# Splitting seventeen weight blocks of the second layer early, and writing the order of every engine out

## The chip, the cores and the metric

The kernel runs on one core of one Trainium2 chip. The metric is the device time of one execution in microseconds, lower is better. The core has five engines that work side by side, each through its own queue in order: TensorE (PE; its weight loads are listed apart as PEld), VectorE (DVE), ScalarE (ACT), GpSimd (POOL) and SyncE (SP), which here issues the transfers. An instruction starts when its engine reaches it and the results that it needs are there.

## The reference

A decoder trunk of two layers on 1024 tokens of 1024 features, all in float32. Each layer has a mixer stage and a feed-forward stage:

```python
for l in range(DEPTH):
    h = rmsnorm(x, attn_norm[l])
    proj = h @ w_in[l]
    (c_q, c_kv, k_r, g_b, g_c, u_conv, u_pool,
     q_sw, k_sw, v_sw) = jnp.split(proj, pts, axis=-1)
    y_a = mla_attention(c_q, c_kv, k_r, ..., w_uq[l], w_ukv[l], cos, sin)
    y_b = short_gated_conv(g_b, g_c, u_conv, conv_w[l])
    y_c = multiscale_pool(u_pool, pool_w[l], pool_scale[l])
    y_d = swa_sink_attention(q_sw, k_sw, v_sw, swa_sinks[l], slopes)
    gf = ... # each group divided by its own root mean square
    x = x + (gf * mix_norm[l]) @ w_o[l]
    h2 = rmsnorm(x, ffn_norm[l])
    gate, up = jnp.split(h2 @ w_gate_up[l], 2, axis=-1)
    x = x + (jax.nn.silu(gate) * up) @ w_down[l]
return rmsnorm(x, final_norm)
```

The four mixers are a latent attention (queries and keys from narrow latents, each with a norm of its own), a gated convolution, pooling over 2 to 16 tokens, and an attention over a window of 128 tokens ("local" below). d_ff is 2816.

## The kernel before

Activations lie transposed: features on the 128 partitions, tokens on the free axis, in two halves t of 512. TensorE is fed with numbers in a shorter format (fp32r), so each float32 operand is split into a high part and the remainder, and a product is three matmuls, high by high, high by low, low by high (`mm3`, line 294 issues them). Splitting is one copy on ACT (line 305, or 308 with a gain) and one subtract on DVE (306 or 309), over tiles of 512 or 1024 columns. Gate and up, down, and part of the input projection of layer 1 use a scheme with seven products of quarter blocks in place of eight. The combined quarters of weights and activations that it needs are worked out ahead on POOL and DVE and kept in DRAM (tiles ws, qd, ad).

The names of tiles in the rows: u is one of 47 slots of 128 x 1024, tn, tp and te are small work tiles, ps_ is PSUM, par holds per-feature gains. A number after a name is a version.

The mixers' weights are loaded in the order in which `expect_layer` lists them. `weights` (line 222) starts a load from the input, then ACT copies (line 237) and DVE subtracts (line 238), into a ring of two pairs of slots.

A norm, `rnorm`, is a chain over four engines: a matmul with ones sums the squares (line 355 or 358), then ACT does Ln (362), Exp (363) and Square (364), DVE corrects (365, 368) and multiplies the input (372), and the result is split (308, 309) and goes to PE. In ACT's queue an ACT_TABLE_LOAD stands ahead of an Ln, Exp or Silu wherever the table set loaded before it in that queue isn't the one for its function. The kernel itself asks for a set of Ln and Exp together, "natural_log_exp_and_others", at its start (line 151) and after each feed-forward (line 1828). The second statement depends on the Silu that the program emitted last:

```python
pl = act.preload_act_table_set("natural_log_exp_and_others")
if pl is not None:
    tc.add_manual_dep(pl.ins, last_silu.ins.name, ...)
```

`swa_unit` works out a block of local attention for two heads: scores in PSUM, maximum with the sink, an exponential on ACT (776), the row's reciprocal on DVE, the scaling of each head's tile by it (791, DVE, 128x256), then transposes and the product with the values.

The feed-forward's loop runs over 22 blocks of 128 gate and 128 up features. The first block is started ahead of the loop proper. `norm(u)` norms half u of the input; `combine` builds the quarters of the activations; `plain_gates`, `plain_silus` and `plain_acts` finish the first block, in plain products, with its Silu on ACT (line 1604) and its two multiplications on DVE. The down projection is a second loop, over 28 units.

What sets the order: the program emits everything in an order of its own, and then a planner (`arrange`) lays out every engine's queue. It goes by estimated durations, ranks and a table MOVES of offsets by line, and by one rule on tables: steps with Silu and steps with Exp or Ln are kept apart, all of one kind ahead of the other. The loads of tables are no steps of the planner; they are put in around its order.

Of the kernel before, what the change touches and what calls it, by code (L numbers as in the profile page):

```python
# [18 lines left out]
P = 128  # L19
# [27 lines left out]
NPL = 1  # L47

# [74 lines left out]
def trunk_kernel(ctx: ExitStack, tc: tile.TileContext, ins, out):  # L123
# [32 lines left out]
    ws = dpool.tile([len(PAIRS), P, 4 * 7 * NQ], F32, name="ws")  # L156
    ad = [dpool.tile([P, NG * HT], F32, name=f"ad{n}") for n in range(7)]
# [82 lines left out]

    def rope_weights(l):

        s = F.half()
        raw = F.ap(s)
        sp.dma_start(raw, ins["w_kr"][l])
        w = R.ap2(ring_next()[0])
        F.free(s)
        rv = raw.rearrange("p (k c) -> p k c", k=NK)
        wv = w.rearrange("p (k h c) -> p k h c", k=NK, h=2)
        act.copy(wv[:, :, 0], rv)  # L250
        dve.tensor_tensor(out=wv[:, :, 1], in0=rv, in1=rd(wv[:, :, 0]), op=ALU.subtract)
        return w
# [6 lines left out]
    def expect_layer(l):  # L259
        for m in (2, 3, 0, 4, 5, 6, 1, 13, 14, 10, 11, 12, None, 7, 8, 9) if l == 0 else (14, 10, 11, 12, None, 7, 8, 9):  # L260
            if m is None:
                expect(rope_weights, l)
            else:
                begin = [first_loads] if (l, m) == (0, 2) else []
                expect(weights, ins["w_in"][l, m], 2 * HT, *begin)
        for d in range(NK):
            expect(weights, ins["w_o"][l, d], 6 * P)
# [241 lines left out]

    factors = {c: [None] * (NK // 2) for c in USES}  # L510
# [65 lines left out]
    for l in range(L):  # L576
# [3 lines left out]
        prep = factor_weights() if l == 0 else iter(())  # L580

# [160 lines left out]
        def swa_unit(g, i):  # L742
# [747 lines left out]
        for n, (h, t) in enumerate(steps):  # L1490
# [27 lines left out]
            if n == 6:  # L1518
# [12 lines left out]
                for k in range(2):  # L1531
                    wa.append(pair_weights(ins["w_oa"][l, k]))
# [190 lines left out]
        combine(1)  # L1723
        plain_gates()
        plain_silus()
        plain_acts()
        norm(1)
# [16 lines left out]
        for f in range(NPL, NFF):  # L1744
# [76 lines left out]
            if f in range(4, 20, 2):  # L1821
                next(prep, None)
        second(*pending)
# [148 lines left out]
MM_NS = {512: 226.7, 384: 173.3, 256: 120.0, 128: 57.0}  # L1972
SIGNAL = {
    "PE": {"PE": 0, "DVE": 37, "ACT": 36, "POOL": 62, "SP": 30},
    "DVE": {"PE": 168, "DVE": 33, "ACT": 33, "POOL": 79, "SP": 27},
    "ACT": {"PE": 165, "DVE": 33, "ACT": 25, "POOL": 77, "SP": 26},
    "POOL": {"PE": 192, "DVE": 33, "ACT": 32, "POOL": 78, "SP": 27},
    "SP": {"PE": 163, "DVE": 35, "ACT": 35, "POOL": 80, "SP": 30},
}
REUSE = {"PE": 153, "DVE": 40, "ACT": 40, "POOL": 40, "SP": 40}  # L1980
OVERLAP = {"DVE": 82, "ACT": 97, "POOL": 44}
SHIFT = {"DVE": 31, "ACT": 24, "POOL": 0}
FUNC_SETS = {"Silu": "Silu", "Exp": "Exp", "Ln": "Exp"}
ENGINES = {"PE": "PE", "DVE": "DVE", "Activation": "ACT", "Pool": "POOL", "SP": "SP"}


class Step:
    __slots__ = ("ins", "eng", "rank", "before", "after", "tiles", "left", "ns", "tail", "ready", "sums", "bank", "onchip", "size", "start", "end", "table", "rows", "place")

    def __init__(self, eng, rank):  # L1990
        self.ins, self.eng, self.rank = [], eng, rank
        self.before, self.after, self.tiles = set(), [], []
        self.ns = self.tail = self.ready = self.size = 0
        self.sums = self.bank = None
        self.onchip = False
        self.table = self.rows = None


def areas(a):
    t = a.bass_ap  # L2000
    shape = [int(n) for n in t.tensor.shape]
    dims = [(int(s), int(n)) for s, n in a.ap]
    off = int(t.offset)
    name = t.tensor.name
    if type(t.tensor).__name__ == "DRamTensorHandle" or name.split("_")[0] in DRAM_TILES:
        row = shape[-1]
        starts, rows, span = [off // row], 1, 1
        for s, n in dims:
            if s == row:
                rows = n  # L2010
            elif s % row == 0 and s:
                starts = [b + k * (s // row) for b in starts for k in range(n)]
            else:
                span += s * (n - 1)
        c = off % row
        return name, [(b, b + rows, c, c + span) for b in starts]
    row = 1
    for n in shape[1:]:
        row *= n
    p, c = divmod(off, row)  # L2020
    span = 1 + sum(s * (n - 1) for s, n in dims[1:])
    return name, [(p, p + dims[0][1], c, c + span)]


DRAM_TILES = {"ws", "xs", "xp", "xr", "qd", "out"} | {f"ad{n}" for n in range(7)}
BUFS = {"ps_mm": 2, "ps_m0": 1, "ps_m1": 1, "ps_s": 3, "ps_t": 2, "ps_pv": 1, "te": 2, "tn": 3, "tp": 3, "vraw": 2, "vhi": 2, "vlo": 2, "sm1": 16, "sm2": 16, "sm16": 2}


def width(a):
    n = 1  # L2030
    for s, k in list(a.ap)[1:]:
        n *= int(k)
    return n


def length(eng, kind, i, ins, outs):
    n = max(width(a) for a in ins + outs)
    ps = any(a.bass_ap.tensor.name.startswith("ps_") for a in ins)
    if eng == "POOL":
        return 206 if kind == "InstMemset" else 177 + 2.18 * n  # L2040
    if eng == "ACT":
        if kind == "InstTensorCopy":
            return 157 + 0.84 * n if ps else 187 + 0.845 * n
        if len(outs) > 1:
            return 261 + 0.836 * n
        if len(ins) > 1 or "Copy" in str(i.func):
            return 261 + 0.836 * n if ps else 294 + 0.83 * n
        return 170 + 0.84 * n if ps else 195 + 0.845 * n
    if kind == "InstCustomDveAnt":
        return 220 + 1.02 * n + 58  # L2050
    if kind == "InstTensorScalarPtr" and not i.is_scalar_tensor_tensor:
        return 152 + 0.53 * n if n < 64 else 215 + 0.514 * n
    if kind == "InstTensorCopy":
        return 150 + 0.52 * n
    if kind == "InstTensorScalarPtr" and len(ins) > 2 and not ps:
        return 212 + 1.04 * n
    return 146 + 1.054 * n


def steps_of(tc):  # L2060
    steps, seen = [], {}
    table, runs = None, {"Silu": [], "Exp": []}
    for i in tc.nc.cur_bb.bb.instructions:
# [4 lines left out]
        ins = [a for a in i.ins if hasattr(a, "bass_ap")]  # L2068
        outs = [a for a in i.outs if hasattr(a, "bass_ap")]
        fp32 = kind == "InstMatmult" and "float32r" not in str(i.ins[1].dtype)  # L2070
        bank = outs[0].bass_ap.tensor.name
        v = steps[-1] if steps else None
        if not (fp32 and v and v.sums and v.bank == bank):
            v = Step(eng, len(steps))
            steps.append(v)
            v.bank, v.sums = bank, fp32
        v.ins.append(i)
        if eng == "PE":
            n = width(outs[0])
            if fp32:  # L2080
                one = i.ins[1].bass_ap.tensor.name.startswith("ones")
                v.ns += {512: 867, 256: 534, 128: 340}[n] if one else 108
                v.tail = 163 if one else 122
            else:
                v.ns = MM_NS[n]
                v.tail = 164 if n > 128 else 173
        elif kind == "InstDMACopy":
            v.size = 4
            for s, n in outs[0].ap:
                v.size *= int(n)  # L2090
            if eng == "POOL":
                v.ns, v.tail = 700, 4200
            elif eng == "ACT":
                v.ns, v.tail = 450, 2400
        else:
            v.ns = length(eng, kind, i, ins, outs)
            if not any(a.bass_ap.tensor.name.startswith("ps_") for a in ins + outs):
                v.onchip = kind != "InstMemset"
            if ins:
                v.rows = tuple(areas(a)[1][0][0] for a in (ins[0], outs[0]))  # L2100
            if eng == "ACT" and len(outs) > 1:
                v.tail = 61
        f = FUNC_SETS.get(str(getattr(i, "func", "")).split(".")[-1])
        if f:
            other = runs["Exp" if f == "Silu" else "Silu"]
            if f != table:
                table = f
                runs[f] = []
            v.before |= set(other)
            runs[f].append(v)  # L2110
            v.table = f
        for a, writes in [(a, False) for a in ins] + [(a, True) for a in outs]:
            name, rects = areas(a)
            if kind == "InstCustomDveAnt":
                rects = [(0, 1 << 30, 0, 1 << 30)]
            if name.startswith("in_"):
                continue
# [856 lines left out]
```

## Time and profile before

| what | value |
|---|---|
| median of 3 runs | 2030.23 us (2029.9 to 2032.06) |
| the profiled execution | 2030.46 us |
| its span, first to last instruction | 2028.2 us |
| granted TensorE clock | 0.998 |
| instructions | 26434 |

The stages in the profiled execution: layer 0's mixers up to about 400 us, its feed-forward to about 810 and its down projection to about 1000; then layer 1 in the same way, its mixers to about 1400. A row of the timeline gives start, length, engine, line, operation, output and inputs, and in brackets how long the engine sat idle before it and what released it. A row of a group gives count, busy time, mean length in ns of one, and idle time before them.

### The profile page before, as it was taken

To read this page: it belongs to the slowest core of one execution; us is meant where nothing else is said; L and a number is where in the kernel's file an instruction comes from. 1 tells how busy PE (TensorE), PEld (TensorE's weight loads), DVE (VectorE), ACT (ScalarE), POOL (GpSimd) and SP (SyncE) were. 2 spreads that over 40 slices of the span, in tenths; PEclk is the share of its full clock that TensorE was granted. 3 is DMA by queue.
4 is the path that set the end of the run, shared out by engine and by line. 5 is a ranking of instruction groups with operands and counts; after the bars stand their busy time and mean duration, and the time that the engine had idled before them with its cause. 6 is when DMAs were issued, how large, how long until landed. Compare 5 with 4: busy or idle time off the path is not lost.

```text
span 2028.2 us, 26434 instructions
## 1 busy us (share of the span) xinstructions
PE 2012.0 (99%) x9378; PEld 1669.8 (82%) x9378; DVE 1641.9 (81%) x2793; ACT 1027.3 (51%) x1803; POOL 195.0 (10%) x212
## 2 busy tenths in 40 slices
PE   9999999999999999999999999999999999999997
PEld 8887888888888888888888878887888888888887
DVE  7889989998888888755778999899877877786455
ACT  6557667753433344544545676667333333354343
POOL 0000000021212212000000000000212222120000
PEclk9999999999999999999999999999999999999999
DMA  5111223346676577866455113231644544498652
GB/s 185 45 37 37 78 83 116 120 156 219 209 231 223 207 238 254 301 226 211 134 163 172 37 45 96 98 128 58 218 143 153 174 162 143 136 319 291 188 191 88
DMA packets 163780, 320.19 MB, mean 158 GB/s; under 512 B 13248, under 2 KB 85056, under 8 KB 163648
## 3 DMA queue, kind: packets, MB, share of 16 engines
q1 hardware_dynamic: 163648, 318.51, 46.8%
q8 instruction: 73, 1.20, 0.2%
q14 instruction: 59, 0.48, 0.1%
HBM read 220.41 MB, written 98.04 MB: 157 GB/s over the span
## 4 chain that ended last, share of the span: by engine, by line
PE 91%; DVE 6%; ACT 1%; issue 1%; DMA 0%; SPq 0%; DVEq 0%; ACTq 0%
PE ps_mm L294 35%; PE ps_s L294 28%; PE ps_t L294 11%; PE ps_pv L294 8%; PE ps_pv L1289 2%; PE ps_t L1277 2%; DVE u L309 1%; DVE u L1408 1%; PE ps_s L1223 1%; PE ps_s L1224 1%; PE ps_s L1225 1%; PE ps_s L753 1%; PE ps_pv L814 1%; DVE u L346 1%; PE ps_mm L1109 1%
## 5 line engine op out<-in xcount | busy, mean ns | idle before, releaser
L294 PE MATMUL ps_mm<-u,u 128*128 128x512 f32 (+1 forms) x3402 | 875.0, 388 | 2.0 <-ACT u L305 1.1
L294 PEld LDWEIGHTS ps_mm<-u,u 128*128 128x128 f32 x3402 | 622.6, 188 | 127.1 <-issue 2.6
L294 PE MATMUL ps_s<-u,u 128*128 128x512 f32 x2628 | 674.0, 389 | 1.2 <-ACT u L305 1.0
L294 PEld LDWEIGHTS ps_s<-u,u 128*128 128x128 f32 x2628 | 492.4, 188 | 105.5 <-ACT u L305 1.7
L305 ACT CAST u<-u 128x1024 fp32r<-128x1024 f32 (+2 forms) x400 | 343.8, 881 | 438.2 <-PE ps_s L294 91.0
L306 DVE TENSOR_TENSOR u<-u,u 128x1024 fp32r<-128x1024 f32 (+2 forms) x400 | 412.5, 1049 | 165.1 <-ACT u L305 122.7
L294 PE MATMUL ps_t<-u,u 128*128 128x512 f32 (+1 forms) x1142 | 297.3, 377 | 0.0
L172 POOL TENSOR_TENSOR u<-u 128x256 f32<-128x256 f32 x176 | 188.8, 1074 | 773.4 <-DMA u<-in_w_dn 370.1
L294 PEld LDWEIGHTS ps_t<-u,u 128*128 128x128 f32 x1142 | 205.6, 188 | 40.4 <-issue 0.5
L294 PE MATMUL ps_pv<-u,u 128*128 128x512 f32 x696 | 194.2, 389 | 0.0
L294 PEld LDWEIGHTS ps_pv<-u,u 128*128 128x128 f32 x696 | 130.3, 188 | 27.5 <-issue 0.4
L1604 ACT ACTIVATE tp<-tp 128x512 f32<-128x512 f32 x84 | 53.0, 632 | 102.5 <-DVE tp L372 102.2
L458 ACT COPY tn<-ps_s 128x512 f32<-128x512 f32 x66 | 38.5, 584 | 99.0 <-PE ps_s L294 98.9
L1286 POOL MEMSET u<- 128x128 f32 x32 | 6.0, 215 | 853.4 <-DVE te L372 618.2
L305 ACT CAST u<-ps_t 128x512 fp32r<-128x512 f32 (+4 forms) x136 | 65.1, 505 | 44.7 <-PE ps_t L1277 27.9
L308 ACT ACTIVATE u<-u,par 128x512 fp32r<-128x512 f32 x100 | 69.4, 717 | 29.8 <-DVE u L372 11.1
L306 DVE TENSOR_TENSOR u<-ps_t,u 128x512 fp32r<-128x512 f32 (+4 forms) x136 | 76.3, 581 | 4.7 <-ACT u L305 3.8
L309 DVE SCALAR_TENSOR_TENSOR u<-u,par,u 128x512 fp32r<-128x512 f32 x100 | 72.4, 744 | 6.8 <-ACT u L308 6.7
L1605 DVE TENSOR_TENSOR tp<-tp,u 128x512 f32<-128x512 f32 x84 | 61.8, 740 | 11.5 <-ACT tp L1604 11.2
L340 ACT ACTIVATE tn<-u 128x512 f32<-128x512 f32 (+1 forms) x92 | 52.6, 594 | 31.0 <-DVE u L1882 17.6
L372 DVE TENSOR_TENSOR tp<-tp,u 128x512 f32<-128x512 f32 x80 | 57.7, 725 | 0.9
L1289 PE MATMUL ps_pv<-u,u 128*128 128x512 f32 (+2 forms) x184 | 52.0, 355 | 0.0
(220 smaller groups left out, 2160.9 us busy)
## 6 DMA issues: line engine op xcount, KB each, us to landing
u<-in_w_gu SPq DMA_DIRECT2D x88, 512.0 KB, 3.9
ad<-u SPq DMA_DIRECT2D x154, 256.0 KB, 2.8
u<-ad SPq DMA_DIRECT2D x70, 512.0 KB, 5.3
u<-in_w_dn SPq DMA_DIRECT2D x68, 512.0 KB, 4.6
qd<-u SPq DMA_DIRECT2D x44, 512.0 KB, 3.0
u<-qd SPq DMA_DIRECT2D x32, 512.0 KB, 4.2
u<-in_w_in SPq DMA_DIRECT2D x29, 512.0 KB, 3.5
u<-ws SPq DMA_DIRECT2D x28, 512.0 KB, 4.0
```

Source lines behind the costliest of these rows:

```text
L172: pool.tensor_tensor(out=o, in0=o, in1=u, op=ALU.add)
L294: pe.matmul(o, w, r, start=start and k == 0 and i == 0, stop=stop and k == n - 1 and i == 2, skip_group_check=again,)
L305: act.copy(hi, f)
L306: dve.tensor_tensor(out=lo, in0=f, in1=rd(hi), op=ALU.subtract)
L308: act.activation(hi, f, AF.Copy, scale=gain)
L309: dve.scalar_tensor_tensor(out=lo, in0=f, scalar=gain, in1=rd(hi), op0=ALU.mult, op1=ALU.subtract)
L340: act.activation(q, f, AF.Square)
L372: dve.tensor_tensor(out=o, in0=a, in1=b, op=ALU.mult)
L1277: pe.transpose(p[:, b * P : (b + 1) * P], pr[b][j // 4][:, (j % 4) * P : (j % 4 + 1) * P], ident,)
L1289: pe.matmul(py[:, c0:], v_of(j, h), R.ap(s)[:, c0:], start=j == 0 and n == 0, stop=j == nj - 1 and n == 1,)
L1604: last_silu = act.activation(g, g, AF.Silu)
L1605: dve.tensor_tensor(out=g, in0=g, in1=r, op=ALU.mult)
```

## The change

Five things change.

1. Seventeen weight blocks of layer 1's mixers (seven of the input projection, the eight of the output projection's first part and the two of its attention part) are no longer split where they are used. `ready_block` reads one, splits it with one copy on ACT and one subtract on DVE, and writes both parts to a DRAM tile wl. It is called for odd f from 3 to 19 in layer 0's feed-forward loop (nine blocks) and for odd n from 5 on in its down projection (eight). In layer 1 `ready_weights` loads the two parts ready-made, with two transfers instead of one.
2. The scaling in `swa_unit` is an ACT copy with a per-row scale instead of a DVE multiplication, in both layers.
3. `norm(1)` stands ahead of `plain_gates`, `plain_silus` and `plain_acts` instead of behind them.
4. The planner, its costs and its table are gone. The order of all five engines is written out as a list of places (ORDER), and `order_engines` makes each instruction follow the one before it in that list. The rule on tables goes with the planner, and table loads are still no part of the list.
5. `expect_layer` and the loading of the attention's output weights use `ready_weights` for layer 1.

The matmuls and their number are the same. Line 362 becomes 375, 363 becomes 376, 305 becomes 318, 1604 becomes 1639 and 1828 becomes 1865.

```diff
+READY = (14, 10, 11, 12, 7, 8, 9) + tuple(("o", d) for d in range(NK)) + (("a", 0), ("a", 1))
...
+    wl = dpool.tile([len(READY), P, 2 * D], F32, name="wl")
...
+    def ready_weights(k, n):
+        pair = ring_next()
+        for j, i in enumerate(pair):
+            sp.dma_start(rd(R.ap2(i)[:, :n]), wl[READY.index(k)][:, j * D : j * D + n])
+        return [R.ap2(i) for i in pair]
...
+            elif l:
+                expect(ready_weights, m, D)
...
+            if l:
+                expect(ready_weights, ("o", d), 6 * P)
+            else:
+                expect(weights, ins["w_o"][l, d], 6 * P)
...
+    def ready_block(k):
+
+        s = F.pair()
+        if isinstance(k, int):
+            src, n = ins["w_in"][1, k], D
+        elif k[0] == "o":
+            src, n = ins["w_o"][1, k[1]], 6 * P
+        else:
+            src, n = ins["w_oa"][1, k[1]], D
+        f = F.ap2(s)[:, :n]
+        sp.dma_start(f, src)
+        h = R.pair()
+        hi = R.ap2(h)[:, :n]
+        act.copy(hi, f)
+        dve.tensor_tensor(out=f, in0=f, in1=rd(hi), op=ALU.subtract)
+        for j, v in enumerate((rd(hi), f)):
+            sp.dma_start(wl[READY.index(k)][:, j * D : j * D + n], v)
+        R.free_pair(h)
+        F.free_pair(s)
...
             for h in range(2):
-                dve.tensor_scalar(
-                    out=p3[:, h, c0:],
-                    in0=p3[:, h, c0:],
-                    scalar1=rs[:, h : h + 1],
-                    scalar2=None,
-                    op0=ALU.mult,
+                act.activation(
+                    p3[:, h, c0:], p3[:, h, c0:], AF.Copy, scale=rs[:, h : h + 1]
                 )
...
         combine(1)
+        norm(1)
         plain_gates()
         plain_silus()
         plain_acts()
-        norm(1)
...
             if f in range(4, 20, 2):
                 next(prep, None)
+            elif blocks_due and f in range(3, 20):
+                ready_block(blocks_due.popleft())
...
+            elif blocks_due and n % 2:
+                ready_block(blocks_due.popleft())
...
+ORDER = {
+    "PE": """
+0 24:2 -26:2 24:2 -26:2 24 -25:2 66 -44 18 24 -25:2 23 -24:3 -24 44 -45:2 -27:3 67 -68:3 21 43
...
+def order_engines(tc):
+
+    info = mybir.DependencyInfo(mybir.DependencyClass.NoSync, mybir.DependencyReason.DATA)
+    queues = {}
+    for eng, _, _, ins in steps_of(tc):
+        queues.setdefault(eng, []).append(ins)
+    for eng, queue in queues.items():
+        places = list(listed(ORDER[eng]))
+        assert sorted(places) == list(range(len(queue)))
+        last = None
+        for n in places:
+            for i in queue[n]:
+                if last:
+                    tc.add_manual_dep(i, last, info, reason="issue order")
+                last = i.name
```

**Where the order moves instructions.** First ACT's queue before, at the start of layer 0's feed-forward; L1604 is the first Silu, L362 and L363 the Ln and Exp of norm(1).

```order
L305 CAST u18_4190<-tp_4176 128x512
L1604 ACT_TABLE_LOAD
L1604 ACTIVATE tp_4193<-tp_4193 128x512
L305 CAST u22_4281<-tp_4273 128x512
L362 ACT_TABLE_LOAD
L362 ACTIVATE tn_4204<-ps_pv_4198 128x512
L305 CAST u24_4292<-u42_3928 128x1024
L363 ACT_TABLE_LOAD
L363 ACTIVATE tn_4204<-tn_4204 128x512
L305 CAST u32_2203<-tp_4274 128x512
```

The same place of ACT's queue now, with L375 and L376 for Ln and Exp and L1639 for the Silu:

```order
L318 CAST u18_4191<-tp_4177 128x512
L318 CAST u24_4293<-u42_3929 128x1024
L375 ACTIVATE tn_4200<-ps_pv_4194 128x512
L376 ACTIVATE tn_4200<-tn_4200 128x512
L318 CAST u22_4282<-tp_4274 128x512
L1639 ACT_TABLE_LOAD
L1639 ACTIVATE tp_4207<-tp_4207 128x512
L318 CAST u32_2204<-tp_4275 128x512
```

Ln and Exp moved ahead of the Silu, and one load stands there where three stood, a fourth, for the next Silu, following further down.

Next the end of layer 0's feed-forward, ACT's queue before; L1828 is the load of the joint set of Ln and Exp.

```order
L1604 ACTIVATE tp_7349<-tp_7349 128x512
L305 CAST u46_7484<-u0_7412 128x1024
L305 CAST u17_7488<-u36_7354 128x512
L305 CAST u9_7553<-u14_7551 128x1024
L1604 ACTIVATE tp_7451<-tp_7451 128x512
L1828 ACT_TABLE_LOAD
L305 CAST u29_7547<-u12_7545 128x1024
```

And now, with L1865 for that load:

```order
L1639 ACTIVATE tp_7515<-tp_7515 128x512
L1865 ACT_TABLE_LOAD
L318 CAST u10_7692<-u41_7628 128x1024
L318 CAST u44_7633<-u21_7418 128x384
L318 CAST u8_7748<-u15_7687 128x1024
L1639 ACT_TABLE_LOAD
L1639 ACTIVATE tp_7413<-tp_7413 128x512
L318 CAST u26_7693<-u30_7565 128x384
```

The Silu that the program emits last (tp_7515) comes ahead of another one (tp_7413), the joint set is loaded between the two, and the Silu's set is loaded again behind it.

Last, the norms of the latents in layer 1, ACT's queue before:

```order
L305 CAST u22_10717<-te_10715 128x512
L362 ACTIVATE tn_10586<-ps_t_10580 128x512
L363 ACTIVATE tn_10586<-tn_10586 128x512
L364 ACTIVATE tn_10587<-tn_10586 128x512
L335 ACTIVATE u24_10668<-u24_10668 128x512
L362 ACTIVATE tn_10657<-ps_t_10655 128x512
L363 ACTIVATE tn_10657<-tn_10657 128x512
L364 ACTIVATE tn_10658<-tn_10657 128x512
```

And now:

```order
L318 CAST u4_10829<-te_10827 128x512
L375 ACT_TABLE_LOAD
L375 ACTIVATE tn_10698<-ps_t_10692 128x512
L376 ACT_TABLE_LOAD
L376 ACTIVATE tn_10698<-tn_10698 128x512
L377 ACTIVATE tn_10699<-tn_10698 128x512
L375 ACT_TABLE_LOAD
L375 ACTIVATE tn_10769<-ps_t_10767 128x512
L348 ACTIVATE u28_10780<-u28_10780 128x512
L376 ACT_TABLE_LOAD
L376 ACTIVATE tn_10769<-tn_10769 128x512
L377 ACTIVATE tn_10770<-tn_10769 128x512
```

The steps of the norms stand in the same sequence, and each Ln and each Exp has a table load ahead of it. Over the whole program ACT's queue holds 11 table loads before and 38 now: one at the start, three in layer 0 and 34 in layer 1, of which 32 belong to the 16 norms.

More of the change, by code (lines that the diff above doesn't have):

```diff
@@ L1 @@
-import heapq
 import math
@@ L1981 @@
[L1981 to L1996, printed above, removed]
@@ L1999, in areas @@
[L1999 to L2022, printed above, removed]
@@ L2025 @@
[L2025 to L2057, printed above, removed]
@@ L2060, in steps_of @@
+ENGINES = {"PE": "PE", "DVE": "DVE", "Activation": "ACT", "Pool": "POOL", "SP": "SP"}
+ORDER = {
+    "PE": """
[172 rows of a table added]
+""",
+    "DVE": """
[76 rows of a table added]
+""",
+    "ACT": """
[46 rows of a table added]
+""",
+    "POOL": """
+0:2 1 -2 2 -2 2 -2 2 -2 1:2 1 -2 1:6 4:2 -6 5 -6:2 4 -5 4:78 1 -2 2 -2 2 -2 1:2 1 -2 1:92
+""",
+    "SP": """
[24 rows of a table added]
+""",
+}
 def steps_of(tc):
-    steps, seen = [], {}
-    table, runs = None, {"Silu": [], "Exp": []}
+    steps = []
     for i in tc.nc.cur_bb.bb.instructions:
@@ L2077, in steps_of @@
[L2077 to L2094, printed above, removed]
-        else:
[L2096 to L2117, printed above, removed]
-            if name.split("_")[0] not in DRAM_TILES and name not in v.tiles:
-                v.tiles.append(name)
-            seen.setdefault(name, [])
-            for r, w, u in seen[name]:
-                cross = name.startswith("ps_") and w == writes
-                if cross or (w or writes) and any(
-                    x[0] < y[1] and y[0] < x[1] and x[2] < y[3] and y[2] < x[3]
-                    for x in r
-                    for y in rects
-                ):
-                    v.before.add(u)
-            seen[name].append((rects, writes, v))
```

197 lines of the change are left out of this document (20 added, 177 removed), and 847 rows, old and new, of tables (MOVES, ORDER).

## The prediction

> **What bounds the kernel now.** The page comes first: its span, the busy shares, ScalarE's slices and the chain by engine.
>
> ```profile
> span 2028.2 us, 26434 instructions
> PE 2012.0 (99%) x9378; PEld 1669.8 (82%) x9378; DVE 1641.9 (81%) x2793; ACT 1027.3 (51%) x1803; POOL 195.0 (10%) x212
> PE 91%; DVE 6%; ACT 1%; issue 1%; DMA 0%; SPq 0%; DVEq 0%; ACTq 0%
> ```
>
> TensorE (PE) is busy for 2012.0 of 2028.2 us and carries 91% of the chain. The change leaves the matmuls as they are, so a gain can only come out of the 16.2 us in which PE does nothing, head and tail of the kernel included. A loss has no such lid: wherever another engine delivers late, PE's idle time grows, and nothing later wins it back. So the question is how much room the other engines have, stage by stage. The next view is busy time by window, in layer 1's mixers (columns: length, then PE, weight loads, DVE, ACT, POOL, clock, DMA share, GB/s).
>
> ```profile
> 1130.00:1160.00 30.00, 30.00 (x172) 25.96 (x170) 29.66 (x89) 25.24 (x65) 0.00 (x0) 1.00 0.13 42
> 1160.00:1197.00 37.00, 37.00 (x158) 28.66 (x157) 35.30 (x61) 29.87 (x52) 0.00 (x0) 1.00 0.10 32
> 1197.00:1218.00 21.00, 20.61 (x98) 17.11 (x97) 21.00 (x40) 12.63 (x25) 0.57 (x2) 1.00 0.15 52
> 1218.00:1240.00 22.00, 21.30 (x106) 17.31 (x107) 22.00 (x52) 16.14 (x40) 0.00 (x0) 1.00 0.20 56
> ```
>
> VectorE (DVE) is full from 1197 to 1240, and PE loses 0.39 + 0.70 = 1.1 us there; two subtracts of weights, of the kind that the change moves away, lie on the chain of waits:
>
> ```profile
> 1201.77 1.21 DVE u L238
> 1217.91 0.86 DVE u L238
> ```
>
> ScalarE (ACT) has 37.00 - 29.87 = 7.1 us free from 1160 to 1197. That window holds the norms of the latent queries, keys and the neighbouring groups. The page's 51% for ACT says nothing about it.
>
> Then the start of layer 0's feed-forward on ACT's timeline (start, length), and PE at the same place and at the same place in layer 1:
>
> ```profile
> 407.73 0.63 ACT L1604 ACTIVATE tp<-tp 128x512 f32<-128x512 f32 x1
> 408.26 0.61 ACT L305 CAST u<-tp 128x512 fp32r<-128x512 f32 x1
> 408.89 1.28 ACT L362 ACT_TABLE_LOAD   x1
> 410.18 0.60 ACT L362 ACTIVATE tn<-ps_pv 128x512 f32<-128x512 f32 x1
> 410.68 1.04 ACT L305 CAST u<-u 128x1024 fp32r<-128x1024 f32 x1
> 411.74 1.28 ACT L363 ACT_TABLE_LOAD   x1
> 413.03 0.63 ACT L363 ACTIVATE tn<-tn 128x512 f32<-128x512 f32 x1
> 413.57 0.60 ACT L305 CAST u<-tp 128x512 fp32r<-128x512 f32 x1
> ```
> ```profile
> 412.58 0.61 PE L294 MATMUL ps_s<-u,u 128*128 128x512 f32 x2
> 414.22 2.14 PE L294 MATMUL ps_s<-u,u 128*128 128x512 f32 x8 [1.03 <-ACT u L305]
> ```
> ```profile
> 1413.28 0.39 PE L294 MATMUL ps_s<-u,u 128*128 128x512 f32 x1
> 1414.73 0.74 PE L294 MATMUL ps_mm<-u,u 128*128 128x512 f32 x2 [1.06 <-ACT u L305]
> ```
>
> This is what a change of function table costs. A 128x512 step normally starts 0.53 us after the one before it (407.73 to 408.26). With a load between them, the Ln starts 410.18 - 408.26 = 1.92 us after the cast: 1.4 us more, for a load of 1.28. After a Silu both Ln and Exp need a load of their own (408.89, 411.74), and the cast behind them reaches PE 1.03 us late. In layer 1's mixers before there is no such load; the view of line 362 (the Ln), from 960 to 1420 us, has one, at 1405.8, in the feed-forward, for 12 + 4 norms:
>
> ```profile
> L362 ACT ACTIVATE tn<-ps_t x12: 577/600/619, 1161.6 to 1352.7; 128x512 f32<-128x512 f32 x12
> L362 ACT ACTIVATE tn<-ps_pv x4: 575/583/599, 1002.4 to 1407.1; 128x512 f32<-128x512 f32 x4
> L362 ACT ACT_TABLE_LOAD  x1: 1283/1283/1283, 1405.8 to 1405.8; - x1
> ```
>
> **The blocks split early.** Layer 1 loses 17 casts on ACT and 17 subtracts on DVE; layer 0's feed-forward and down projection get them, with 51 DMAs, and 17 more DMAs go to layer 1. The dearest pair of rows is
>
> ```profile
> L237 ACT CAST u<-u 128x1024 fp32r<-128x1024 f32 x21 | 21.7, 1045 | 4.7 <-PE ps_mm L294 2.5 <-DMA u<-in_w_in 1.8 <-issue 0.4
> L238 DVE TENSOR_TENSOR u<-u,u 128x1024 fp32r<-128x1024 f32 x21 | 25.5, 1220 | 7.7 <-PE ps_t L294 4.7 <-ACT u L237 1.8 <-PE ps_pv L814 0.9
> ```
>
> so at most 17 x 1.05 = 17.8 us of ACT and 17 x 1.22 = 20.7 us of DVE move. Where they arrive there is room:
>
> ```profile
> 720.00:760.00 40.00, 40.00 (x178) 33.08 (x178) 33.72 (x46) 15.66 (x22) 8.98 (x9) 1.00 0.71 239
> 840.00:880.00 40.00, 40.00 (x179) 33.10 (x178) 24.25 (x28) 19.67 (x24) 0.00 (x0) 1.00 0.82 285
> ```
>
> A block about every 36 us of the feed-forward puts 1.2 us on a DVE with 6.3 of 40 free, and 1.5 MB on DMA engines with 0.29 of their time free. I cost this at nothing; PE's work on other weights hides it, and without that cover it would be DVE's 1.2 us a block. SP is passed in order, so its weight loads queue behind the writes, which wait for the subtract; stores of combinations already queue there in the same way. In layer 1 the subtracts leave the full DVE: I credit all of the 1.1 us that PE loses from 1197 to 1240, with bounds of 0 and 1.1.
>
> **The scaling on ACT.** Layer 1 scales 32 tiles. The nearest ACT row for one, with a per-row operand and the same columns, is the exponential's:
>
> ```profile
> L776 ACT ACTIVATE tp<-ps_s,sm 128x256 f32<-128x256 f32 x56 | 26.3, 473 | 13.7 <-DVE sm L763 6.6 <-DVE sm L789 3.2 <-DVE sm L372 2.9
> ```
>
> 32 x 0.47 = 15 us on ACT. The attention lies beside the window 1130 to 1160, where 4.8 us are free and casts of projection weights leave at 1.05 each. I take nothing, because casts out and scales in are alike; the bounds are 0 and 2 us.
>
> **norm(1) ahead of the Silus.** In layer 0 Ln and Exp then still find the first table: four loads become one, and the 1.03 us at 414.22 goes. In layer 1 Ln and Exp do load, for the reason below, so its 1.06 us stays.
>
> **The written order.** This is the dear term. At the end of layer 0's feed-forward, the order (its rows are shown with the change) puts the load of line 1865, a set with both Ln and Exp, ahead of the last Silu. The Silu's own table is loaded again behind it, so layer 1 starts on the Silu set, and every one of its 16 norms loads twice: 32 loads at 1.4 us are 44.8 us of ACT. What reaches PE, place by place:
>
> - A, 1160 to 1197. Seven norms lie there, which is 14 loads and 19.6 us:
>
> ```profile
> L362 ACT ACTIVATE tn<-ps_t 128x512 f32<-128x512 f32 x7 | 4.2, 596 | 1.5 <-PE ps_t L355 1.1 <-PE ps_t L358 0.4
> ```
>
> ACT has 7.1 us free and loses one cast of 1.05: 19.6 - 8.2 = 11.4 us late. The casts in that queue feed PE, which is busy all 37.00 us, so I take it whole (bounds 5.7, if half is taken up next door, and 19.6).
> - B, two more norms, 4 loads or 5.6 us. From the first Ln to the split behind the second one ACT's timeline has a single gap:
>
> ```profile
> 1220.60 0.62 ACT L362 ACTIVATE tn<-ps_t 128x512 f32<-128x512 f32 x1
> 1226.35 0.59 ACT L305 CAST u<-ps_t 128x512 fp32r<-128x512 f32 x1 [0.47 <-PE ps_t L1277]
> 1230.23 0.71 ACT L308 ACTIVATE u<-u,par 128x512 fp32r<-128x512 f32 x1
> ```
>
> So 5.6 - 0.5 = 5.1 us (bounds 0, if the 5.9 us free until 1240 take it, and 5.6).
> - C, the attention output's norms. The later one is the tightest chain of the layer: ones matmul, Ln, Exp, DVE, split, PE.
>
> ```profile
> 1352.68 0.60 ACT L362 ACTIVATE tn<-ps_t 128x512 f32<-128x512 f32 x1 [0.20 <-PE ps_t L355]
> 1356.83 1.16 ACT L340 ACTIVATE tn<-u 128x512 f32<-128x512 f32 x2 [0.47 <-DVE u L368]
> 1358.03 1.95 ACT L308 ACTIVATE u<-u,par 128x512 fp32r<-128x512 f32 x3
> 1359.09 0.62 PE L294 MATMUL ps_s<-u,u 128*128 128x512 f32 x2
> ```
>
> The split's first tile ends near 1358.8 and PE starts on it at 1359.09. Two loads, 2.8 us, less the idle 0.20 and 0.47, make 2.1 late; the earlier norm I take at nothing (bounds 0 and 5.6 for both).
> - D, the start of layer 1 (Ln at 1002.4): loads between casts that PE waits for, as at 414.22, so 1.0 (bounds 0 and 2.1).
>
> The three norms left over are one near 1200 and two at the feed-forward's start, where loads stood before too; I take nothing for them.
>
> [...]
>
> **The sum.** A + B + C + D = 11.4 + 5.1 + 2.1 + 1.0 = 19.6 us lost; 1.03 + 1.1 = 2.1 won; net +17.5. The profiled execution took 2030.46 us (span plus 2.3), 0.2 above the median, so 2048.0. Bounds: 5.7 lost and 2.1 won give 2034; all upper bounds (19.6 + 5.6 + 5.6 + 2.1 = 32.9, 2 for the scales, nothing won) give 2065.
>
> **Rivals.**
> 1. ACT takes the loads up. A load needs no operand, so it may run while ACT waits for the ones matmul, and the rows that the order moves may give PE other work meanwhile. Place: A. Price: the losses shrink to nothing and the gains stay, 2028.4, within 0.2%. It decides if fewer than 6 of the 44.8 us reach PE. For it speaks that the four windows above leave ACT 4.8 + 7.1 + 8.4 + 5.9 = 26 us free, as much as the 18 loads of A and B take; against it, that 14 of them crowd into 37 us with 7.1 free. If the relieved DVE gives back a further 2 us of PE's idle time too, it is 2026, just faster.
> 2. All 32 loads land on PE. Each stands in a chain that PE waits for, and DVE, behind ACT in the queue, gets late as well: 2030.46 + 44.8 - 2.1 = 2073. Against it: those 26 free us of ACT.
> 3. The transfers of the early blocks hold up layer 0's down projection. At 840 to 880 the DMA engines are busy for 0.82 of 40 us, 7.2 us free. Two blocks of 384 KB, read once and written twice, are 2.3 MB, or at 285 GB/s for a share of 0.82 (347 GB/s full) 6.6 us. It fits narrowly. If not, weights come late by up to 5 us over the stage, on top: 2053.
>
> **How the numbers follow.** My forecast has 0.79, rival 1 has 0.12 (0.08 within 0.2%, 0.04 below), rival 2 has 0.05, rival 3 has 0.04. About what a measurement tells from no change is 0.2%, 4 us: 2026.2 to 2034.3. Of the forecast 0.03 falls inside it, at its low end. So faster 0.04, same 0.11, slower 0.79 - 0.03 + 0.05 + 0.04 = 0.85. The range is 2034 to 2064: it leaves out rival 1, rival 2 and the outermost of the bounds.
>
> **What would show it.** The changed kernel's profile should hold 38 table loads, 32 of them at the Ln and Exp of layer 1's norms; ACT without gaps where A stands, and PE gaps there released by ACT, 9 to 14 us in sum; some 5 us at B; no gap at the start of layer 0's feed-forward. Layer 0 until its down projection ends should be as long as before within 2 us. I am wrong if PE has no ACT gaps at A, if a switch takes another time than 1.4 us, or if the time is lost in layer 0 instead.

## The result and the profile after

The changed kernel takes 2077.16 us (median of 5, 2076.53 to 2078.32) against 2030.23, a ratio of 1.023 with an interval of 1.0215 to 1.0245: 47 us slower. I had forecast slower, 2048.0, in a range of 2034 to 2064. The profiled execution took 2078.32 us. Its page begins:

```profile
span 2076.3 us, 26535 instructions
PE 2027.1 (98%) x9378; PEld 1674.1 (81%) x9378; DVE 1645.4 (79%) x2729; ACT 1086.2 (52%) x1894; POOL 194.6 (9%) x212
PE 86%; DVE 5%; ACT 5%; DMA 2%; issue 1%; SPq 0%; DVEq 0%; ACTq 0%
```

Two things are to be seen. ACT's share of the chain went from 1% to 5%. And PE, with the same matmuls, is busy for 2027.1 us instead of 2012.0, so a part of the loss isn't idle time. The table loads are there. These groups of ACT (count, busy time and mean ns, idle time before them) hold 31 of the 32 loads that belong to layer 1's norms; the other stands at an exponential of the attention, which runs between the last Ln and Exp of the latents' norms.

```profile
L375 ACT ACT_TABLE_LOAD x16 | 20.5, 1283 | 4.5 <-DVE u L381 3.6 <-PE ps_t L368 0.6
L376 ACT ACT_TABLE_LOAD x15 | 19.2, 1283 | 0.3
```

The three windows of layer 1's mixers on which the forecast rested (length; PE, weight loads, DVE, ACT, POOL; clock; DMA). They are the same times as before, not the same work, because the changed kernel falls behind in them:

```profile
1160.00:1197.00 37.00, 32.45 (x126) 24.45 (x124) 24.87 (x41) 33.54 (x50) 0.00 (x0) 0.86 0.17 53
1197.00:1218.00 21.00, 17.36 (x72) 12.74 (x71) 14.34 (x23) 19.18 (x27) 0.00 (x0) 1.00 0.19 63
1218.00:1240.00 22.00, 18.86 (x81) 14.50 (x80) 18.88 (x38) 13.26 (x25) 0.00 (x0) 1.00 0.11 37
```

DVE, full or nearly so here before, is now idle for 3 to 12 us of each window, PE waits too, and ACT is the fullest engine of the first two. The clock changed as well: 0.86 in the first window, 1.00 before. ACT's timeline and PE's at that place:

```profile
1178.23 1.28 ACT L375 ACT_TABLE_LOAD   x1
1179.52 0.60 ACT L375 ACTIVATE tn<-ps_t 128x512 f32<-128x512 f32 x1
1180.14 1.28 ACT L376 ACT_TABLE_LOAD   x1
1181.43 0.63 ACT L376 ACTIVATE tn<-tn 128x512 f32<-128x512 f32 x1
1182.09 0.63 ACT L377 ACTIVATE tn<-tn 128x512 f32<-128x512 f32 x1
1182.74 1.28 ACT L375 ACT_TABLE_LOAD   x1
```
```profile
1182.78 0.84 PE L1139 MATMUL ps_mm<-u,u 128*128 128x512 f32 x3
1185.67 1.12 PE L371 MATMUL ps_t<-u,ones 128*128 128x512 f32 x2 [2.05 <-DVE u L350]
1186.23 1.71 PE L307 MATMUL ps_mm<-u,u 128*128 128x512 f32 x3
```

Load follows load. PE waits 2.05 us. Three matmuls of 128x512 took 0.84 us ahead of the wait, three of the same shape take 1.71 behind it, and the granted clock is 0.50 from 1187 to 1193. The windows around the three places where that happens ahead of PE's last matmul give the most that it can have cost, as length times the clock that is missing: 18 x 0.28 = 5.0, 20 x 0.09 = 1.8 and 20 x 0.17 = 3.4 us. It is an upper bound, because PE stood idle for a part of the slow stretches: in the last one the clock is 0.50 from 2023.20 on, and PE's next matmul is at 2024.84.

```profile
1176.00:1194.00 18.00, 15.35 (x43) 10.56 (x44) 10.88 (x18) 17.26 (x22) 0.00 (x0) 0.72 0.04 7
1440.00:1460.00 20.00, 16.26 (x64) 12.70 (x64) 17.28 (x26) 15.12 (x24) 0.00 (x0) 0.91 0.03 7
2015.00:2035.00 20.00, 13.88 (x98) 13.67 (x97) 8.52 (x15) 3.40 (x8) 0.00 (x0) 0.83 0.13 34
```

The view of PE's waits shows something that I hadn't looked for (total, times, longest):

```profile
PE ps_t L307 <- DVE u L1919: 7.2, 2, 6.1
PE ps_mm L307 <- ACT u L318: 4.1, 2, 3.7
```

The longest wait, 6.1 us, isn't in the norms at all. It stands at 2024.84, at the end of layer 1's down projection, where the kernel before has no gap of PE.

### The profile page after: what moved, and what is told of

Its sections match the earlier page's. It is cut to its first block, busy times and chain, and to the rows that moved or that the text cites. A ratio compares the mean times of both kernels' runs of the same rounds, so it can differ in the third digit from the quotient of the medians.

```text
span 2076.3 us, 26535 instructions
## 1 busy us (share of the span) xinstructions
PE 2027.1 (98%) x9378; PEld 1674.1 (81%) x9378; DVE 1645.4 (79%) x2729; ACT 1086.2 (52%) x1894; POOL 194.6 (9%) x212
## 4 chain that ended last, share of the span: by engine, by line
PE 86%; DVE 5%; ACT 5%; DMA 2%; issue 1%; SPq 0%; DVEq 0%; ACTq 0%
PE ps_mm L307 34%; PE ps_s L307 26%; PE ps_t L307 10%; PE ps_pv L307 7%; DVE u L319 2%; PE ps_pv L1319 2%; PE ps_t L1307 1%; ACT u L318 1%; DMA u<-qd 1%; ACT L375 1%; ACT L376 1%; PE ps_s L1253 1%; PE ps_s L1255 1%; PE ps_s L1254 1%; PE ps_s L787 1%
## 5 line engine op out<-in xcount | busy, mean ns | idle before, releaser
L307 PE MATMUL ps_mm<-u,u 128*128 128x512 f32 (+1 forms) x3402 | 938.0, 390 | 9.9 <-ACT u L318 4.1
L307 PE MATMUL ps_s<-u,u 128*128 128x512 f32 x2628 | 704.1, 389 | 1.4 <-ACT u L239 0.9
L307 PE MATMUL ps_t<-u,u 128*128 128x512 f32 (+1 forms) x1142 | 322.7, 382 | 8.3 <-DVE u L1919 7.2
L1639 ACT ACTIVATE tp<-tp 128x512 f32<-128x512 f32 x84 | 52.8, 632 | 84.2 <-DVE tp L385 84.2
L319 DVE TENSOR_TENSOR u<-ps_t,u 128x512 fp32r<-128x512 f32 (+4 forms) x136 | 78.4, 584 | 11.9 <-ACT u L318 10.2
L321 ACT ACTIVATE u<-u,par 128x512 fp32r<-128x512 f32 x100 | 69.0, 716 | 28.8 <-DVE u L385 13.7
L1640 DVE TENSOR_TENSOR tp<-tp,u 128x512 f32<-128x512 f32 x84 | 63.5, 759 | 12.2 <-ACT tp L1639 11.5
L385 DVE TENSOR_TENSOR tp<-tp,u 128x512 f32<-128x512 f32 x80 | 60.9, 763 | 1.1
L1319 PE MATMUL ps_pv<-u,u 128*128 128x512 f32 (+2 forms) x184 | 57.3, 356 | 0.0
```

The lines of the kernel that those rows point to most:

```text
L307: pe.matmul(o, w, r, start=start and k == 0 and i == 0, stop=stop and k == n - 1 and i == 2, skip_group_check=again,)
L319: dve.tensor_tensor(out=lo, in0=f, in1=rd(hi), op=ALU.subtract)
L321: act.activation(hi, f, AF.Copy, scale=gain)
L385: dve.tensor_tensor(out=o, in0=a, in1=b, op=ALU.mult)
L1319: pe.matmul(py[:, c0:], v_of(j, h), R.ap(s)[:, c0:], start=j == 0 and n == 0, stop=j == nj - 1 and n == 1,)
L1639: last_silu = act.activation(g, g, AF.Silu)
```

## The experiments

Theory L: the table loads are the main cause. Rival W: the written order and the moved blocks are. "Before" is the kernel before, timed on the same chip each time, 2030.15 to 2030.32 us.

**e1_table**: the loads taken out of the changed kernel. The joint set's load is made to follow the last four Silus that were emitted, so that it comes behind both.

```diff
             last_silu = act.activation(g, g, AF.Silu)
+            silus.append(last_silu)
...
-            tc.add_manual_dep(
-                pl.ins,
-                last_silu.ins.name,
+            for si in silus[-4:]:
+                tc.add_manual_dep(
+                    pl.ins,
+                    si.ins.name,
```

> The changed kernel with one edit: the load of the joint Ln/Exp set after layer 0's feed-forward also follows the other last Silus, so that 5 table loads are left of 38. Theory L (the loads are the main cause): PE's extra idle time from layer 1's start to its feed-forward goes, some 33 us, and the time is near 2044. Rival W (the written order and the moved blocks cost the time, the loads fall beside it): under 12 us come back, 2065 or more. In both, what is lost in layer 0's feed-forward and down projection (7 us) and at the end (10 us) stays.

Measured: 2039.49 us, 1.0045 of before (1.003 to 1.006). So 37.7 us come back, more than the 19.6 of my sum and the 33 that I expected here, and 9 remain. Since this kernel and the changed one have the same order, the same matmul can be looked up in both. These are the first matmuls with ones at D, A, B, C and the feed-forward's start, in the timeline of the changed kernel, then of e1_table:

```profile
1008.57 0.39 PE L368 MATMUL ps_pv<-u,ones_r 128*128 128x512 f32 x1
1167.43 0.40 PE L368 MATMUL ps_t<-u,ones_r 128*128 128x512 f32 x1
1242.80 0.62 PE L368 MATMUL ps_t<-u,ones_r 128*128 128x512 f32 x2
1365.80 0.40 PE L368 MATMUL ps_t<-u,ones_r 128*128 128x512 f32 x1
1421.47 0.61 PE L368 MATMUL ps_pv<-u,ones_r 128*128 128x512 f32 x2
```
```profile
1006.89 0.39 PE L368 MATMUL ps_pv<-u,ones_r 128*128 128x512 f32 x1
1162.49 0.39 PE L368 MATMUL ps_t<-u,ones_r 128*128 128x512 f32 x1
1219.24 0.61 PE L368 MATMUL ps_t<-u,ones_r 128*128 128x512 f32 x2
1337.00 0.40 PE L368 MATMUL ps_t<-u,ones_r 128*128 128x512 f32 x1
1389.07 0.62 PE L368 MATMUL ps_pv<-u,ones_r 128*128 128x512 f32 x2
```

The lead of e1_table is 1.7 us when layer 1 starts, then 4.9, 23.6, 28.8 and 32.4, and it is 39.3 at the end of the span (2076.3 against 2037.0). So the loads cost 1.7 us in layer 0 (where the two loads between its last Silus stand), 3.3 at D, 18.6 at A, 5.2 at B, 3.6 at C and 6.9 behind, nearly all at the feed-forward's start.

**e2_noload**: the loads put into the kernel before. The line that loads the joint set is left out for layer 0.

```diff
-        pl = act.preload_act_table_set("natural_log_exp_and_others")
+        pl = act.preload_act_table_set("natural_log_exp_and_others") if l else None
```

> The kernel before with one edit: no load of the joint set after layer 0's feed-forward, so that 28 loads come in ahead of the Ln and Exp of 14 norms of layer 1, in the planner's order. Theory L: 28 loads cost here what they cost in the changed kernel or a little less, 25 to 35 us, so 2055 to 2065. Rival W: the planner's order has room for them, under 10 us, at most 2040.

Measured: 2066.94 us, 1.0182 of before (1.0167 to 1.0197), 36.8 us more, a little above theory L's range. It holds 40 loads in place of 11: 30 came in at the Ln and Exp of 15 norms (I had expected 14 norms), and the joint set's own went. The groups, which had two loads each before, and the window of A:

```profile
L362 ACT ACT_TABLE_LOAD x17 | 21.8, 1283 | 0.9 <-PE ps_t L355 0.6
L363 ACT ACT_TABLE_LOAD x17 | 21.8, 1283 | 0.3
1160.00:1197.00 37.00, 28.46 (x110) 21.27 (x109) 25.22 (x41) 30.88 (x42) 0.00 (x0) 0.91 0.04 15
```

The planner's order has no more room for them than the written one: 1.3 us of time for each of the 29 loads more. Rival W falls as the main cause, though the other 9 us speak for it.

**e3_tail** and **e5_end**: the wait near the end. In the changed order, DVE's subtract of u1_17674 stands ahead of two others, but its ACT copy comes behind one that waits for PE; SP's next load waits for a slot that one of the two frees. In the changed kernel's chain that load (line 1700) is issued at 2016.64, 0.02 us behind DVE's line 319, and its transfer takes 5.63 us. And PE's order there reads

```
L307 MATMUL ps_t_16888<-u7_17657,u15_17727 128x256 x3
L307 MATMUL ps_t_16888<-u33_17522,u31_17726 128x256
L307 MATMUL ps_t_16888<-u10_17523,u31_17726 128x256
L307 MATMUL ps_t_16888<-u33_17522,u46_17728 128x256
L307 MATMUL ps_t_16888<-u33_17522,u31_17726 128x256
L307 MATMUL ps_t_16888<-u10_17523,u31_17726 128x256
L307 MATMUL ps_t_16830<-u33_17522,u40_17673 128x256
```

The first row ends the first half of PSUM tile 16888, which DVE has to read; five matmuls of its second half follow at once, and only then the other tile. e3_tail moves the subtract, e5_end also the five matmuls:

```diff
         places = list(listed(ORDER[eng]))
+        if eng == "DVE":
+            places.insert(2538, places.pop(2536))
+        if eng == "PE":
+            early = places[8780:8785]
+            del places[8780:8785]
+            k = places.index(8949)
+            places[k:k] = early
```

> As e1_table, and one subtract of DVE's order in layer 1's down projection (the low part of u1_17674) moved behind the two after it. Theory T: the 6.1 us that PE waits near the end come from this subtract, which stands ahead of the one that frees the slot for SP's next load; 8 to 10 us less than e1_table (with the half clock that follows the wait), near 2035. Rival: the last weights come late from the DMA queue whatever DVE does; the same as e1_table within 2 us.

> As e3_tail, and in the PE order of the last stage five matmuls moved: the first five of the second half of PSUM tile ps_t_16888, which stand right behind its first half, now stand behind the first half of ps_t_16830. Theory P: PE waits there (3.7 us in e3_tail, and 3.4 us of half clock behind it) because it returns to a tile whose first half DVE still has to read, while the order before goes on with the other tile; 6 to 8 us less than e3_tail, near 2030.5. Rival: the tiles' inputs come late too, so the wait moves to the other tile; 2036 to 2038.

Measured: e3_tail 2037.97 us (1.002 to 1.0049 of before), only 1.5 less than e1_table, which the spread of the runs hardly tells from nothing. e5_end 2032.35, 1.0007 of before (0.9998 to 1.0016). PE at the place, in the changed kernel, in e1_table, in e3_tail and in e5_end:

```profile
2014.61 4.11 PE L307 MATMUL ps_t<-u,u 128*128 128x256 f32 x33
2024.84 5.36 PE L307 MATMUL ps_t<-u,u 128*128 128x256 f32 x24 [6.12 <-DVE u L1919]
```
```profile
1975.78 4.11 PE L307 MATMUL ps_t<-u,u 128*128 128x256 f32 x33
1984.99 7.21 PE L307 MATMUL ps_t<-u,u 128*128 128x256 f32 x36 [5.10 <-DVE u L1921]
```
```profile
1978.25 4.11 PE L307 MATMUL ps_t<-u,u 128*128 128x256 f32 x33
1986.05 4.15 PE L307 MATMUL ps_t<-u,u 128*128 128x256 f32 x20 [3.69 <-DVE u L1921]
```
```profile
1975.65 7.59 PE L307 MATMUL ps_t<-u,u 128*128 128x256 f32 x62
1983.45 4.70 PE L307 MATMUL ps_t<-u,u 128*128 128x256 f32 x37 [0.21 <-DVE u L1921]
```

The wait to start from is e1_table's, 5.10 us. With DVE's order mended it shrinks to 3.69; with PE's order mended as well it is 0.21. From the first row shown to the end of the span, which leaves out what differs earlier, e1_table takes 61.2 us, e3_tail 58.7 and e5_end 53.7. So theory T explained a part and theory P the larger rest, each less than it promised (8 to 10 and 6 to 8); by the medians the two together are worth 7.1 us. This is the written order's own fault: with the loads gone, 5.10 of the 6.12 us still stand.

**e4_quiet** and **e6_small**: what the early blocks cost in layer 0. The first, on e1_table, cuts their writes; the second, on e5_end, cuts reading, copy, subtract and writes. Layer 1 loads one block's parts for all in both, and so works with wrong weights. Their edits, beside those of e1_table and e5_end:

```diff
+            m = n if k == READY[0] else 64
-            sp.dma_start(wl[READY.index(k)][:, j * D : j * D + n], v)
+            sp.dma_start(wl[READY.index(k)][:, j * D : j * D + m], v[:, :m])
```
```diff
+        if k != READY[0]:
+            n, src = 64, src[:, :64]
         f = F.ap2(s)[:, :n]
...
-            sp.dma_start(rd(R.ap2(i)[:, :n]), wl[READY.index(k)][:, j * D : j * D + n])
+            sp.dma_start(rd(R.ap2(i)[:, :n]), wl[0][:, j * D : j * D + n])
```

> As e1_table, with the traffic of the early blocks cut: only the first block is written to DRAM in full, of the other sixteen only 64 columns of each part, and layer 1 loads the first block's parts in place of all of them (so layer 1 computes with wrong weights). The instructions and their order are the same. Theory D: the 7 us lost in layer 0's feed-forward and down projection come from the DMA engines being full; 4 to 7 us less than e1_table, near 2039. Rival: they come from ACT's and DVE's extra work and from the order; the same as e1_table within 1.5 us.

> As e5_end, with sixteen of the seventeen early blocks cut to 64 columns: reading, copy, subtract and both writes (layer 1 loads the first block's parts for all, so it computes with wrong weights). Instructions and order stay. Theory B: the 7 us still lost in layer 0's feed-forward and down projection are the blocks' own work on ACT, DVE and the DMA engines; 5 to 7 us less than e5_end. Rival: they come from the written order there (DVE ahead of PE, weights asked for late); at most 2 us less.

Measured: e4_quiet 2037.99 us against e1_table's 2039.49, e6_small 2030.87 against e5_end's 2032.35. Both are 1.5 us less, and in both pairs the intervals against before overlap. Theories D and B, which wanted 4 to 7, fall. The blocks' work and traffic in layer 0 cost 1.5 us at most by these medians.

**e7_scale**: e5_end with the scaling put back on DVE. The lists follow: the places of the scalings leave ACT's, and each pair stands behind its reciprocal in DVE's.

```diff
-                act.activation(
-                    p3[:, h, c0:], p3[:, h, c0:], AF.Copy, scale=rs[:, h : h + 1]
-                )
+                SCALED.append(dve.tensor_scalar(
+                    out=p3[:, h, c0:],
+                    in0=p3[:, h, c0:],
+                    scalar1=rs[:, h : h + 1],
+                    scalar2=None,
+                    op0=ALU.mult,
+                ).ins.name)
```

> As e5_end, with the local attention's scaling back on DVE, each pair of multiplications behind its reciprocal in DVE's order. My prediction took the scaling on ACT at nothing (0 to 2 us either way); that makes e5_end within 1 us. Rival: the scaling on ACT is what frees the full DVE in the mixers; then this is 2 to 5 us slower than e5_end.

Measured: 2039.31 us, 1.0045 of before (1.0031 to 1.0059), 7.0 more than e5_end. PE's waits hold entries that e5_end's lack, the local attention's product among them:

```profile
PE ps_pv L850 <- DVE u L321: 1.4, 4, 0.7
PE ps_t L838 <- DVE u L691: 0.5, 1, 0.5
```

The two make 1.9 of the 7.0 us; where the rest lies isn't shown. It is the price of undoing the move in an order laid out for it, and no gain over the kernel before: there the scaling is on DVE too, in an order made for that, and PE has no idle time in layer 1's local attention. The window in the kernel before, then in e7_scale:

```profile
1080.00:1150.00 70.00, 70.00 (x364) 58.81 (x363) 68.61 (x181) 44.16 (x111) 0.00 (x0) 1.00 0.34 104
1080.00:1150.00 70.00, 68.44 (x343) 55.87 (x342) 64.27 (x161) 34.04 (x88) 0.00 (x0) 1.00 0.46 143
```

**e8_more**: e5_end with two more places of DVE's order mended, at 635 and at 822 us.

```diff
             places.insert(2538, places.pop(2536))
+            places.insert(1180, places.pop(1178))
+            places[965], places[966] = places[966], places[965]
```

> As e5_end, with two subtracts of DVE's order moved: near 635 us the split that PE waits for goes ahead of a sum of weight quarters, and near 822 the split of a down weight goes behind the multiplication that frees a PSUM tile. Theory O: the time still lost in layer 0 comes from single places of the written order; the waits of 1.1 and 0.9 us at 635 and 822 go, 1.5 to 2.5 us less than e5_end, about 2030. Rival: the next instruction is late just as much; no change within 1 us.

Measured: 2028.94 us, 0.9995 of before (0.9986 to 1.0003), 3.4 less than e5_end, though the two intervals overlap. PE's waits at the two places, 1.12 and 0.86 us in e5_end, are gone, as theory O has it. It is the best version of all, and not to be told from before.

**e9_norm**: norm(1) ahead of the Silus, alone, in the kernel before.

```diff
+        norm(1)
         plain_gates()
         plain_silus()
         plain_acts()
-        norm(1)
```

> The kernel before, with norm(1) alone put ahead of the first block's Silus, in the planner's order; 5 table loads in place of 11. My prediction gave the move 1.03 us in layer 0 and left layer 1's 1.06 in place because the loads came back there. Theory L: here both waits at the feed-forwards' starts go, 2 to 3 us less than before, 2027.5. Rival: the norm's place on DVE and PE costs as much as the loads did; no change within 1 us.

Measured: 2039.8 us, 1.0043 of before (1.0029 to 1.0057): 9.5 slower, and both theories miss. The loads and the wait at 413 us are gone, but the planner lays the copies out otherwise, and PE waits longer, 12 us later:

```profile
422.53 1.14 ACT L305 CAST u<-tp 128x512 fp32r<-128x512 f32 x2 [3.47 <-PE ps_s L294]
425.11 1.89 ACT L305 CAST u<-tp 128x512 fp32r<-128x512 f32 x3 [0.91 <-DVE tp L438]
```
```profile
425.78 0.73 PE L294 MATMUL ps_s<-u,u 128*128 128x512 f32 x2 [3.06 <-ACT u L305]
427.00 1.22 PE L294 MATMUL ps_s<-u,u 128*128 128x512 f32 x2 [0.48 <-DVE u L306]
```

The two matmuls at 427.00 take 1.22 us, where two of the same shape took 0.62 at 418.03: a slow stretch again, behind waits of 3.06 and 0.48 us. So the move alone doesn't pay in the planner's order; in the written one PE has no wait there.

## Why the prediction was wrong

The direction, the main cause and the place of most of the loss were right; the size was off by 29 us. Two steps of the sum failed. The larger is the one from 44.8 us of loads on ACT to 19.6 us late on PE, which let ACT's free time take up more than half: e1_table shows 37.7 us. The smaller is that the written order was taken to cost nothing but its loads: e3_tail and e5_end show 7.1 us at the end alone. Term by term:

- **Term A**, 11.4 forecast, 18.6 measured. PE's waits there, from 1167 to 1243 us, add up to 11.2 us, inside the 9 to 14 of my sign, but ACT releases only 3.6 of them and DVE, behind ACT in the chain, 7.6. What the term lacked altogether is the half clock behind the waits, up to 5.0. I also counted seven norms and set the eighth, near 1200, at nothing; it loads in the same queue, so by my own sum it should have been 16 x 1.4 - 8.2 = 14.2. With the half clock that is 19.2, near what was measured, but this sum was made afterwards and its parts weren't tested apart.
- **Term B**, 5.1 forecast, 5.2 measured.
- **Term C**, 2.1 forecast, 3.6 measured: "the earlier norm I take at nothing" was wrong: PE waits 1.22 us at 1372.55 behind the earlier norm and 1.09 at 1387.55 behind the later.
- **Term D**, 1.0 forecast, 3.3 measured. I took the wait at 414.22 as a model of it. There are four loads at D, 5.6 us, and more than half of them arrives.
- **The feed-forward's start in layer 1**, nothing forecast, 6.9 measured. I argued that loads stood there before too. But there two norms and a Silu load five times now, and PE's timeline shows 3.74 us of wait at 1449.55, with up to 1.8 of half clock behind it.
- **The end**, nothing forecast, 7.1 measured. This is the second failed step. No table load is near 2024.84. I had looked at the order where the norms stand, and not where PE ran without a gap before.
- **Layer 0**, as long as before within 2 us by my sign. It isn't: by 1000 us PE has begun 20 matmuls fewer than before, some 4 us of work at 1000 / 4590 = 0.22 us each, and e1_table 13 fewer (4577), some 3 us. The first row is the kernel before, the second the changed one. So a part of the time was lost in layer 0, most of it with the loads gone too, and at most 1.5 us of it by the early blocks. Two of the places in the written order are those of e8_more, which has 4592.

```profile
0.00:1000.00 1000.00, 996.40 (x4590) 825.31 (x4591) 824.58 (x1400) 521.09 (x904) 95.90 (x108) 1.00 0.50 167
0.00:1000.00 1000.00, 993.16 (x4570) 821.01 (x4571) 835.67 (x1375) 541.84 (x944) 100.15 (x108) 1.00 0.56 188
```

- **The gains**, 2.1 forecast. They are there once the loads are gone. The wait at 414.22 did go, and from 1000 to 1460 us PE, which lost 2.36 us before, has no idle time at all in e1_table (below, before and e1_table). Which of the changes brings that wasn't tested apart. That the scaling gains nothing over before isn't refuted by e7_scale's 7.0, which is a price within the written order.

```profile
1000.00:1460.00 460.00, 457.64 (x2212) 379.01 (x2211) 420.68 (x872) 292.69 (x602) 15.67 (x28) 1.00 0.34 110
1000.00:1460.00 460.00, 460.00 (x2229) 382.00 (x2228) 404.69 (x828) 289.60 (x618) 14.95 (x28) 1.00 0.39 128
```

- **The early blocks** at nothing in layer 0: right within 1.5 us. What they bring layer 1 alone wasn't measured.
- **Rival 1** rested on a load that runs while ACT waits. In the kernel before, a load that the kernel itself asks for did that: line 1828's at 1811.47 ends 0.54 us before PE releases the cast behind it. At layer 1's norms every function starts within 0.02 us of its load's end. The timeline at 1438 us, where ACT was idle longest ahead of a norm's load, shows the opposite: the load starts only when the wait ahead of the Ln is over, released by DVE's line 381, which reads a tn tile as the Ln writes one.

```profile
1437.47 0.68 DVE L381 SCALAR_TENSOR_TENSOR u<-tn 128x512 f32<-128x512 f32 x1
1438.26 1.28 ACT L375 ACT_TABLE_LOAD   x1 [3.59 <-DVE u L381]
```

So ACT's free time there didn't take up the load, and the 7.1 us that I subtracted at A may have been worth less than they looked. **Rival 2**, all loads on PE, 2073, was the nearest, and 0.05 was far too little for it: 33 loads fewer gave back 37.7 us, 1.14 each, and 29 loads more cost 36.8, 1.3 each, the half clock included. That its time is so near is partly luck, since the loads cost 37.7 and not 44.8, and the order that it left out made up the difference. **Rival 3** didn't happen: without the blocks' traffic e4_quiet is only 1.5 us shorter than e1_table.

The rows from 1178.23 to 1182.74 again have 1.28 us of load, and the Ln and the Exp start 0.01 us behind it. From the cast at 1177.59 to the Ln at 1179.52 are 1.93 us, 1.4 more than the 0.53 of two steps without a load, so a switch took what I had priced it at. The early load of the joint set brought layer 1's 32 loads in, and e1_table, which puts it behind the last Silus, is 37.7 us shorter.

The account of the 46.9 us, by the runs: 37.7 the loads (e1_table), 7.1 the order of the last stage (e3_tail and e5_end), and 2.1 left over. The 2.1 is a net: it holds the gains of the change and what the written order still costs in other places. Two more of these are worth 3.4 (e8_more), which ends 1.4 below before and can't be told from it.

## What to carry to other kernels

When an order is written out or replaced, count what stands around it in the profile, table loads above all (38 here in place of 11), and look at every place where the expensive engine was without a gap before, not only at those the change names. Price a wait on a full TensorE with the slow stretch that can follow it (here at most 10.2 us in all). A dependency on "the last one emitted" is not one on the last one in the queue.

## What the hardware showed that I had not expected

TensorE's granted clock fell behind waits, and once within one: three matmuls took 1.71 us instead of 0.84 at 1186.23, and the three windows lost at most 5.0 + 1.8 + 3.4 = 10.2 us together, a fifth of the whole difference. Not every wait brings it: at 1205 PE waited longer than at 1185, and the window from 1197 to 1218 shows a clock of 1.00.

```profile
1175.85 0.50 PE L368 MATMUL ps_t<-u,ones_r 128*128 128x512 f32 x1 [1.90 <-ACT u L318]
1205.12 1.13 PE L371 MATMUL ps_t<-u,ones 128*128 128x512 f32 x2 [2.48 <-DVE tn L378]
```

The clock is 0.50 from 1177 to 1180, from 1187 to 1193 and from 1450 to 1453, behind waits of 1.90, 2.05 and 3.74 us, and from 2023.20 to 2029, which begins within the wait of 6.12. So a wait of 2.05 us was followed by it and one of 2.48 wasn't. What decides it wasn't tried.

The longest idle time of ACT ahead of a norm's load, 3.59 us at 1438.26, gave the load no cover: it started when that wait was over, and the Ln followed it at once, at 1439.55.
